# A hybrid conformer/attention trunk: layer norm statistics in two parts, a moved constant table, reordered silus and sums, and eight more taps on GpSimd

## The chip, the core and the metric

The kernel runs on one core of a Trainium2 chip. A core has five engines that each take their own instructions in order: TensorE (PE, matrix products), VectorE (DVE), ScalarE (ACT), GpSimd (POOL) and SyncE (SP, which here only issues transfers). They meet through semaphores, so an instruction that waits holds up everything behind it on its engine. The metric is the device time of one execution in microseconds, lower is better.

## What is computed

Two layers on a 512 x 1024 float32 activation. Layer 0 is a causal conformer convolution module and a SwiGLU feed-forward; layer 1 is sliding-window attention with shared keys and values and a second feed-forward; a final RMS norm follows. Only the convolution module and the start of the first feed-forward matter here:

```python
def conformer_conv(x, w_pw1, b_pw1, w_dw, b_dw, ln_g, ln_b, w_pw2, b_pw2):
    a = jax.nn.glu(x @ w_pw1 + b_pw1, axis=-1)
    y = lax.conv_general_dilated(
        a, w_dw[:, None, :].astype(a.dtype), window_strides=(1,),
        padding=((CONV_WIDTH - 1, 0),),
        dimension_numbers=('NWC', 'WIO', 'NWC'),
        feature_group_count=D_MODEL) + b_dw
    y = jax.nn.silu(layernorm(y, ln_g, ln_b))
    return y @ w_pw2 + b_pw2

h = h + conformer_conv(rmsnorm(h, norm_mix[l]), ...)
h = h + swiglu_ffn(rmsnorm(h, norm_ffn[l]), ffn_w_up[l], ffn_w_down[l])
```

The convolution is depthwise: each of the 1024 channels has 31 taps over the time axis. The layer norm goes over the 1024 channels. Layer 1's attention adds a relative-position bias, made from two small inputs (`sinks` and `rel_bias`).

## The kernel before

Channels lie on the 128 partitions in 8 channel tiles, tokens on the free axis. The convolution module is worked in two halves of 256 tokens (`hf` 0 and 1).

**The projection loop.** A `Pw1` (L546) is one channel tile of one half: 16 float32 matmuls of 256 columns (L555) into one PSUM bank, 8 for the linear part and 8 for the gate. After two tiles worked ahead, `projs` (L757) runs over the six remaining tiles of the first half (`at_` 0 to 5) and the eight of the second (`at_` 6 to 13). A tile's `gate` is a sigmoid on ACT (L564) and a product on DVE into the padded buffer `apad` (L569).

**The taps.** `Half.taps` (L579) convolves a tile. Of its 31 taps, `N_POOL` go the way ACT then POOL: ACT scales the shifted input into a buffer `pr` (first tap L594, others L596, eight buffers) and POOL adds it to the running sum (L597). The rest are multiply-adds on DVE (L602 for the first, L604). POOL adds the two sums into `y` (L608). Tiles are worked in four pairs (0 to 3); a step of `conv` is one DVE tap of both tiles of a pair with the ACT/POOL taps that fall to it.

**The statistics.** After pair 0, `shift_rows` (L621) forms a row of minus the mean of its channels with two matmuls (L624); it is the start of the DVE sum of later tiles, and is added to `y` of tiles 0 to 3 (L631). `squares` squares a pair's `y` on ACT (L633), `sums` adds `y` and its squares over partitions with four matmuls (L642). When all pairs are in, `scales` (L645) copies the sums on ACT (L647), turns them with four one-column matmuls (L650), forms mean and variance on DVE (L652 to L657), the power -0.5 on POOL (L659) and four diagonal blocks on ACT (L664); `spread` (L666) is one matmul that spreads them over the partitions (L668). `rows` (L670) then makes `z`: two DVE operations a tile (L680, L681) and a silu on ACT (L682).

**The order around it.** A list `follow` (L758) says after which projection what is issued. The first half's taps are spread over `at_` 0 to 10; from `at_` 10 on the second half's steps are taken early, `N_EARLY` (L527) of them a projection. The rest of the second half is a generator (`background`, L687), paid out as a `job` over the weight chunks of what follows: `pw2` (L707) of the first half, then its feed-forward `ffn_part`. `issue_after` fixes an earliest place in an issue order that a scheduler with its own timing then lays down; on the chip each engine follows that order.

**What follows on PE.** `pw2` is 64 float32 matmuls (L253), which take `z` tile by tile. Its evacuation gives `h` (L714) and the split input of the feed-forward, `x` as a high and a low part (L375 on ACT, L376 on DVE) with squares for the RMS norm (L329 on ACT, L333 on POOL). The feed-forward's products are three matmuls each (L255 to L257) with weights that are split as well: L203 on ACT (`whi`), L204 on DVE (`wlo`), from `raw` buffers that SP loads. Its RMS scale runs L343 on PE, L345 on DVE, L347 on POOL, L355 on ACT, L368 on PE.

**The bias constants.** `table` (L724) issues three small loads on SP's queue (`sk`, `lhs`, `oh`), a matmul (L730), two ACT operations (L731 on its result, L732 on `sk`) and a 3 MB store `fd`, which is read back much later for the attention bias.

Of the kernel before, what the change touches and what calls it, by code (L numbers as in the profile page):

```python
# [12 lines left out]
AF = mybir.ActivationFunctionType  # L13
ALU = mybir.AluOpType
# [21 lines left out]
LAST = (9, 11)  # L36
N_POOL = ((13, 13, 12, 12), (13, 17, 17, 17))

# [111 lines left out]
def hybrid_trunk(ctx: ExitStack, tc: tile.TileContext, xT, W, prm_in, wdw_in, sinks, relb, onehot, outT):  # L150
# [375 lines left out]
    N_RAW = 2  # L526
    N_EARLY = (5, 5, 8, 4)  # L527
    raw = [x[:, HALF[1]] for x in xg]
# [12 lines left out]
    with tc.tile_pool(name="conv", bufs=2) as cv:  # L541
# [29 lines left out]
        class Half:  # L571
            def __init__(self, hf, after=()):
                self.hf, self.after, self.last = hf, after, ()
                self.y = quads.tile([P, KT, W2], F32, tag="quad", name=uid("y"))
                self.shift = None
                self.st = None
                self.n_steps = sum(TAPS - n + 1 for n in N_POOL[hf]) + KT + 8

# [65 lines left out]

            def scales(self):  # L645
                row = temp()
                self.copied = nc.scalar.copy(row, self.st).ins  # L647
                pt = bank()
                for n in range(4):
                    nc.tensor.matmul(pt[:, n:n + 1], row[:, n * P:(n + 1) * P], ident[:, 0:1], start=n == 0, stop=n == 3)  # L650
                mv = small.tile([P, 2], F32, tag="mv", name=uid("mv"))
                nc.vector.tensor_scalar(mv, pt[:, 0:2], 1.0 / D, None, op0=ALU.mult)  # L652
                m2 = small.tile([P, 2], F32, tag="m2", name=uid("m2"))
                nc.vector.tensor_mul(m2, pt[:, 0:2], mv)
                nc.vector.tensor_sub(pt[:, 4:6], pt[:, 2:4], m2)
                var = small.tile([P, 2], F32, tag="var", name=uid("var"))
                nc.vector.tensor_scalar(var, pt[:, 4:6], 1.0 / D, EPS, op0=ALU.mult, op1=ALU.add)  # L657
                rr = small.tile([P, 2], F32, tag="rr", name=uid("rr"))
                nc.gpsimd.tensor_tensor(rr, var, mhalf[:, 0:2], op=ALU.pow)  # L659
                self.dg = temp()  # L660
                for n, c in enumerate((mv, rr)):
                    for e in range(2):
                        b = (2 * n + e) * P
                        self.spreads = nc.scalar.mul(self.dg[:, b:b + P], ident, c[:, e:e + 1]).ins  # L664
# [5 lines left out]
            def rows(self, split_z):  # L670
# [7 lines left out]
                for i in range(KT):  # L678
                    t = temp()[:, 0:W2] if split_z else self.z[i]
                    nc.vector.tensor_sub(t, self.y[:, i, :], pb[:, 0:W2])  # L680
                    nc.vector.tensor_mul(t, t, pb[:, W2:2 * W2])  # L681
                    nc.scalar.activation(t, t, AF.Silu, scale=col("lng", i), bias=col("lnb", i))  # L682
                    if split_z:
# [3 lines left out]
            def background(self):  # L687

                gen = self.conv()
                for p in range(KT // 2):  # L690
                    for _ in range(TAPS - N_POOL[self.hf][p] + 1):
                        next(gen)
                        yield
                    if p == 0:
                        self.shift_rows()
                        yield
                    self.squares(p)
                    yield
                    self.sums(p)
                yield  # L700
                self.scales()
                yield
# [20 lines left out]

        def table():  # L724
            nc.sync.dma_start(sk, sinks.to_broadcast([P, NH]))
            nc.sync.dma_start(lhs[0:NBUCKET, :], relb)
            nc.sync.dma_start(oh, onehot)
            nc.gpsimd.memset(lhs[NBUCKET:NBUCKET + 1, :], NEG)
            pf = bank()
            nc.tensor.matmul(pf[0:NH, 0:3 * P], lhs, oh, start=True, stop=True)  # L730
# [26 lines left out]
        projs = [(0, ct) for ct in range(N_RAW, KT)] + [(1, ct) for ct in range(KT)]  # L757
        follow = {2: [rms1.step1, table], 4: [lambda: norm_x(rms1, HALF[1]), h0.shift_rows]}  # L758
        for p, at_ in enumerate((5, 7, 9, 10)):
            follow.setdefault(at_, []).append(lambda p=p: h0.squares(p))  # L760
            follow.setdefault(at_ + 1, []).append(lambda p=p: h0.sums(p))
        follow[11].append(h0.scales)
        done, early, late = 0, 0, None
        for at_, (hf, ct) in enumerate(projs):
            proj = Pw1(hf, ct, mid=h0.spread if at_ == 13 else None)
            if late is not None:
# [4 lines left out]
            if hf == 0:  # L771
                proj.gate()
            while done < n_taps * min(1, (at_ + 1) / 11):
                next(taps, None)
                done += 1
            for f in follow.get(at_, ()):
                with tc.issue_after(proj.last[1 if f is h0.scales or at_ < 11 else 0]):
                    f()
# [3 lines left out]
            if at_ >= 10:  # L782

                with ExitStack() as st:
                    for ins in (gated, h0.copied if at_ == 12 else None, h0.spreads if at_ == 13 else None):
                        if ins is None:
                            continue
                        st.enter_context(tc.issue_after(ins))
                    for _ in range(N_EARLY[at_ - 10]):
                        next(second)  # L790
                        early += 1
        late.gate()
        for _ in h0.rows(False):
            pass
        base = seen[0]
        job(second, h1.n_steps - early, base, base + 44)
        x0 = {"ffn0": Act(KT)}
# [331 lines left out]
```

## Time and profile before

| | us |
|---|---|
| median of 3 runs | 1135.4 (1133.58 to 1135.97) |
| profiled execution | 1135.46 |
| its span, first to last instruction | 1133.7 |
| PE busy in the span | 1108.3 (98%) |
| DVE, ACT, POOL busy | 668.6, 512.2, 325.3 |
| PE idle in the span | 25.4 |
| mean granted PE clock | 0.993 |

1.8 us of the profiled execution lie outside its span. Times in the trace count from the span's start. In a timeline, rows of an engine give start, length, engine, line, operation, output and input, the count, and in brackets the idle time before with what ended it. In the view by windows, the count in brackets is of instructions that touch the window, and PEclk is the granted clock of TensorE as a share of full speed.

### The profile page before, as it was taken

What the parts mean: (1) busy time and instruction counts of PE and PEld (TensorE: products, weight loads), DVE (VectorE), ACT (ScalarE), POOL (GpSimd) and SP (SyncE); (2) the same over time, 40 slices, a digit from 0 to 9 for tenths busy, and PEclk for the clock granted to TensorE, in tenths of its full rate; (3) what the DMA queues carried; (4) which work ended last, traced back from release to release, by engine and by line L of the source; (5) the groups of instructions that cost most, each with busy time, mean ns of one, the idle gap of its engine ahead of it and who ended that gap; (6) DMA issues with size and microseconds to landing.
All of it is one profiled execution on the core that took longest, in us unless ns stands there. A gap on an engine that the chain in (4) does not pass through costs nothing.

```text
span 1133.7 us, 16111 instructions
## 1 busy us (share of the span) xinstructions
PE 1108.3 (98%) x6140; PEld 963.3 (85%) x6140; DVE 668.6 (59%) x1068; ACT 512.2 (45%) x902; POOL 325.3 (29%) x429
## 2 busy tenths in 40 slices
PE   9999898999999999999999999999999999999997
PEld 7888787899999998888878777888888888888887
DVE  4799788896865553454464675765444333444355
ACT  3787677845554433232352574643332212222234
POOL 3899689910010001121220232332111100111014
PEclk9999998999999999999999999999999999999998
DMA  9380034467555653333323211113323333233322
GB/s 362 105 97 4 9 106 165 133 203 242 171 184 185 186 175 105 93 93 101 103 75 99 85 41 38 38 56 98 107 93 93 97 106 95 93 93 97 108 91 97
DMA packets 41722, 128.16 MB, mean 113 GB/s; under 512 B 4491, under 2 KB 12844, under 8 KB 41644
## 3 DMA queue, kind: packets, MB, share of 16 engines
q1 hardware_dynamic: 40924, 126.56, 36.4%
q8 instruction: 48, 0.79, 0.3%
q10 hardware_dynamic: 720, 0.57, 0.2%
q14 instruction: 30, 0.25, 0.1%
HBM read 121.87 MB, written 5.24 MB: 112 GB/s over the span
## 4 chain that ended last, share of the span: by engine, by line
PE 77%; DVE 8%; issue 4%; ACT 4%; POOL 4%; DMA 3%; SPq 0%; POOLq 0%; DVEq 0%; ACTq 0%
PE bank L255 25%; PE bank L256 25%; PE bank L257 24%; DVE bank L604 4%; POOL pr L597 3%; PE bank L900 1%; ACT pr L596 1%; DMA w<-in_W_dram 1%; DVE quad L376 1%; DMA sk<-in_sinks_dram 1%; PE bank L921 1%; ACT whi L203 1%; DMA h<-in_xT_dram 1%; DVE wlo L204 1%; ACT z L682 0%
## 5 line engine op out<-in xcount | busy, mean ns | idle before, releaser
L256 PE MATMUL bank<-quad,whi 128*128 128x512 f32 (+1 forms) x1584 | 543.5, 343 | 2.4 <-DVE quad L376 2.4
L257 PE MATMUL bank<-quad,wlo 128*128 128x512 f32 (+1 forms) x1584 | 543.1, 343 | 1.8 <-DVE wlo L204 1.8
L255 PE MATMUL bank<-quad,whi 128*128 128x512 f32 (+1 forms) x1584 | 544.0, 345 | 0.3
L204 DVE TENSOR_TENSOR wlo<-raw,whi 128x1024 fp32r<-128x1024 f32 x200 | 269.8, 1349 | 318.5 <-ACT whi L203 309.7
L203 ACT CAST whi<-raw 128x1024 fp32r<-128x1024 f32 x200 | 209.6, 1048 | 361.8 <-PE bank L256 315.2
L256 PEld LDWEIGHTS bank<-quad,whi 128*128 128x128 f32 x1584 | 301.0, 190 | 38.6 <-DVE quad L376 3.7
L257 PEld LDWEIGHTS bank<-quad,wlo 128*128 128x128 f32 x1584 | 300.9, 190 | 36.8 <-DVE wlo L204 2.4
L255 PEld LDWEIGHTS bank<-quad,whi 128*128 128x128 f32 x1584 | 300.9, 190 | 36.5 <-ACT quad L939 0.6
L465 POOL TENSOR_TENSOR tmp<-tmp,tmp 128x512 f32<-128x512 f32 x32 | 45.6, 1427 | 485.1 <-DVE tmp L464 471.5
L597 POOL TENSOR_TENSOR pr<-pr,pr 128x256 f32<-128x256 f32 x212 | 161.0, 798 | 10.1 <-ACT pr L596 9.9
L604 DVE SCALAR_TENSOR_TENSOR bank<-apad,wdw,bank 128x256 f32<-128x256 f32 x244 | 113.6, 486 | 4.5
L555 PE MATMUL bank<-quad,w 128*128 128x256 f32 x512 | 113.7, 381 | 1.0 <-DMA w<-in_W_dram 0.7
L596 ACT ACTIVATE pr<-apad,wdw 128x256 f32<-128x256 f32 x212 | 102.3, 503 | 26.0 <-POOL pr L597 22.3
L555 PEld LDWEIGHTS bank<-quad,w 128*128 128x128 f32 x512 | 96.5, 190 | 17.0 <-DVE quad L530 3.2
L333 POOL TENSOR_TENSOR tmp<-tmp,tmp 128x256 f32<-128x256 f32 (+1 forms) x42 | 44.9, 1068 | 129.7 <-ACT tmp L329 103.6
L463 ACT ACTIVATE tmp<-tmp 128x512 f32<-128x512 f32 x32 | 20.1, 632 | 86.4 <-DVE tmp L462 86.4
L914 POOL TENSOR_SCALAR sc<-sc,sm 128x256 f32<-128x256 f32 (+1 forms) x64 | 30.6, 499 | 86.2 <-DVE sm L912 86.1
L376 DVE SCALAR_TENSOR_TENSOR quad<-h,prm,quad 128x512 fp32r<-128x512 f32 (+1 forms) x40 | 42.6, 1096 | 1.9 <-ACT quad L375 1.8
L379 ACT CAST quad<-tmp 128x512 fp32r<-128x512 f32 (+1 forms) x48 | 27.8, 585 | 29.5 <-POOL tmp L465 25.6
L464 DVE TENSOR_TENSOR tmp<-bank,rsbc 128x512 f32<-128x512 f32 x32 | 22.1, 691 | 30.4 <-PE bank L257 30.4
L910 ACT ACTIVATE sc<-sc,m 128x257 f32<-128x257 f32 (+1 forms) x64 | 30.2, 475 | 15.2 <-DVE m L903 14.5
L380 DVE TENSOR_TENSOR quad<-tmp,quad 128x512 fp32r<-128x512 f32 (+1 forms) x48 | 30.9, 651 | 2.3 <-ACT quad L379 2.3
(136 smaller groups left out, 754.3 us busy)
## 6 DMA issues: line engine op xcount, KB each, us to landing
raw<-in_W_dram SPq DMA_DIRECT2D x208, 512.0 KB, 3.5
w<-in_W_dram SPq DMA_DIRECT2D x15, 512.0 KB, 9.7
fd<-fs SPq DMA_DIRECT2D x1, 3072.0 KB, 33.8
h<-in_xT_dram SPq DMA_DIRECT2D x8, 256.0 KB, 5.6
bias<-fd SPq DMA_DIRECT2D x8, 256.0 KB, 5.7
out_dram<-res SPq DMA_DIRECT2D x13, 128.0 KB, 1.8
w<-in_W_dram SPq DMA_DIRECT2D x2, 256.0 KB, 4.0
out_dram<-res ACTq DMA_DIRECT2D x3, 128.0 KB, 2.4
```

Of the source, the lines that this page charges most:

```text
L203: nc.scalar.copy(hi, r)
L204: lo_engine[0].tensor_sub(lo, r, f32(hi))
L255: nc.tensor.matmul(out, w[0], x[0], start=start, stop=False)
L256: nc.tensor.matmul(out, w[0], x[1], start=False, stop=False)
L257: nc.tensor.matmul(out, w[1], x[0], start=False, stop=stop)
L333: self.eng.tensor_add(sq, self.acc, sq)
L376: nc.vector.scalar_tensor_tensor(dst[1], src, g, f32(dst[0]), op0=ALU.mult, op1=ALU.subtract)
L465: nc.gpsimd.tensor_mul(t2, t1, t2)
L555: mm = nc.tensor.matmul(self.pb[:, w * W2:(w + 1) * W2], w1[ct][:, w, k, :], x[k] if x else xg[k][:, tok], start=k == 0, stop=k == KT - 1)
L596: on_act = nc.scalar.mul(pr, a[:, j:j + W2], tap(j))
L597: on_pool = nc.gpsimd.tensor_add(pr, acc, pr)
L604: on_dve = nc.vector.scalar_tensor_tensor(yt if i == nd - 1 else c, src, tap(i), c if i else self.shift, op0=ALU.mult, op1=ALU.add)
```

## The change

It has five parts.

1. `table` is cut in two. `table_in` (the three loads and a memset) stays where `table` was, at `at_` 2; the matmul, the two ACT operations and the store move to `at_` 6, behind the sigmoid of the first half's last gate.
2. `scales` is cut into `scales_a` (copy, one-column matmuls, mean and variance) and `scales_b` (power and diagonal blocks), with second-half steps between; the `spread` comes ahead of all 16 matmuls of projection 13 and no longer between its halves.
3. The last gate of the second half moves behind the eight silus of the first half's `rows`, and the second half's further taps come behind them too.
4. In the second half, `shift_rows`, `squares` and `sums` of a pair are issued 3, 4 and 8 steps into the next pair, no longer at once; `N_EARLY` goes from (5, 5, 8, 4) to (7, 3, 4, 2), and the job's span from 44 to 42 weight chunks.
5. Pair 0 of the second half gives 17 taps a tile to ACT and POOL, before 13.

```diff
-N_POOL = ((13, 13, 12, 12), (13, 17, 17, 17))
+N_POOL = ((13, 13, 12, 12), (17, 17, 17, 17))
-    N_EARLY = (5, 5, 8, 4)
+    N_EARLY = (7, 3, 4, 2)
-            def scales(self):
+            def scales_a(self):
                 row = temp()
                 self.copied = nc.scalar.copy(row, self.st).ins
...
-                nc.vector.tensor_scalar(var, pt[:, 4:6], 1.0 / D, EPS, op0=ALU.mult, op1=ALU.add)
+                self.varied = nc.vector.tensor_scalar(var, pt[:, 4:6], 1.0 / D, EPS, op0=ALU.mult, op1=ALU.add).ins
+                self.mv, self.var = mv, var
+
+            def scales_b(self):
+                mv, var = self.mv, self.var
                 rr = small.tile([P, 2], F32, tag="rr", name=uid("rr"))
...
             def background(self):
                 gen = self.conv()
+                due = []
                 for p in range(KT // 2):
-                    for _ in range(TAPS - N_POOL[self.hf][p] + 1):
+                    for s in range(TAPS - N_POOL[self.hf][p] + 1):
                         next(gen)
+                        while due and due[0][0] <= s:
+                            due.pop(0)[1]()
                         yield
-                    if p == 0:
-                        self.shift_rows()
-                        yield
-                    self.squares(p)
+                    due = [(3, self.shift_rows)] if p == 0 else []
+                    due += [(4, lambda p=p: self.squares(p)), (8, lambda p=p: self.sums(p))]
+                for _, f in due:
+                    f()
                     yield
-                    self.sums(p)
+                self.scales_a()
                 yield
-                self.scales()
+                self.scales_b()
+                yield
                 yield
                 yield
                 self.spread()
                 yield from self.rows(True)
...
-        def table():
+        def table_in():
             nc.sync.dma_start(sk, sinks.to_broadcast([P, NH]))
             nc.sync.dma_start(lhs[0:NBUCKET, :], relb)
             nc.sync.dma_start(oh, onehot)
             nc.gpsimd.memset(lhs[NBUCKET:NBUCKET + 1, :], NEG)
+
+        def table():
             pf = bank()
...
-        follow = {2: [rms1.step1, table], 4: [lambda: norm_x(rms1, HALF[1]), h0.shift_rows]}
+        follow = {2: [rms1.step1, table_in], 4: [lambda: norm_x(rms1, HALF[1]), h0.shift_rows], 6: [table]}
...
-        follow[11].append(h0.scales)
+        follow[11].append(h0.scales_a)
         for at_, (hf, ct) in enumerate(projs):
-            proj = Pw1(hf, ct, mid=h0.spread if at_ == 13 else None)
+            if at_ == 13:
+                with tc.issue_after(proj.last[1]):
+                    spread = h0.spread()
+            with tc.issue_after(spread) if at_ == 13 else nullcontext():
+                proj = Pw1(hf, ct)
...
-                    for ins in (gated, h0.copied if at_ == 12 else None, h0.spreads if at_ == 13 else None):
+                    for ins in (gated, h0.copied if at_ == 11 else None, h0.varied if at_ == 11 else None, h0.spreads if at_ >= 12 else None):
...
+            if at_ == 11:
+                h0.scales_b()
-        late.gate()
         for _ in h0.rows(False):
             pass
+        with tc.issue_after(h0.silu):
+            late.gate()
+        h1.after = [h0.silu]
         base = seen[0]
-        job(second, h1.n_steps - early, base, base + 44)
+        job(second, h1.n_steps - early, base, base + 42)
```

More of the change, by code (lines that the diff above doesn't have):

```diff
@@ L576, in __init__ @@
                 self.st = None
-                self.n_steps = sum(TAPS - n + 1 for n in N_POOL[hf]) + KT + 8
+                self.n_steps = sum(TAPS - n + 1 for n in N_POOL[hf]) + KT + 7
             def taps(self, ct, c):
@@ L681, in rows @@
                     nc.vector.tensor_mul(t, t, pb[:, W2:2 * W2])
-                    nc.scalar.activation(t, t, AF.Silu, scale=col("lng", i), bias=col("lnb", i))
+                    self.silu = nc.scalar.activation(t, t, AF.Silu, scale=col("lng", i), bias=col("lnb", i)).ins
                     if split_z:
@@ L776, in hybrid_trunk @@
             for f in follow.get(at_, ()):
-                with tc.issue_after(proj.last[1 if f is h0.scales or at_ < 11 else 0]):
+                with tc.issue_after(last_sig) if f is table else nullcontext(), tc.issue_after(proj.last[1 if f == h0.scales_a or at_ < 11 else 0]):
                     f()
```

1 line of the change is left out of this document (added).

## The prediction

> **What bounds the kernel now.** I read the page, then the busy time by windows, then the timelines of each engine around the windows where PE is not full.
>
> ```profile
> span 1133.7 us, 16111 instructions
> PE 1108.3 (98%) x6140; PEld 963.3 (85%) x6140; DVE 668.6 (59%) x1068; ACT 512.2 (45%) x902; POOL 325.3 (29%) x429
> ...
> 260.00:600.00 340.00, 339.14 (x2132) 308.07 (x2132) 191.70 (x222) 138.56 (x183) 38.64 (x31) 1.00 0.45 142
> ...
> 770.00:1100.00 330.00, 330.00 (x1464) 273.19 (x1463) 135.84 (x143) 91.80 (x106) 31.73 (x23) 1.00 0.31 98
> ```
>
> The columns are PE, PEld, DVE, ACT, POOL, PEclk, DMA. PE is the bound; what the change touches ends near 275, and no matmul is added or removed. So only PE's idle time and lowered clock before that can be won, or grow:
>
> ```profile
> 50.00:60.00 10.00, 8.83 (x41) 7.12 (x40) 9.46 (x25) 8.52 (x19) 10.00 (x15) 1.00 0.58 67
> ...
> 130.00:140.00 10.00, 8.27 (x35) 6.12 (x34) 4.34 (x13) 9.04 (x16) 9.50 (x14) 1.00 0.01 2
> 140.00:150.00 10.00, 8.27 (x29) 6.34 (x29) 9.51 (x23) 9.99 (x23) 7.35 (x11) 0.83 0.23 73
> ...
> 170.00:180.00 10.00, 7.63 (x50) 6.38 (x48) 8.63 (x14) 9.17 (x21) 10.00 (x12) 0.92 0.68 256
> 180.00:190.00 10.00, 10.00 (x58) 9.51 (x58) 7.99 (x11) 6.25 (x11) 10.00 (x11) 0.74 0.36 107
> 190.00:200.00 10.00, 8.06 (x66) 7.80 (x65) 7.69 (x14) 7.21 (x14) 10.00 (x13) 1.00 0.33 106
> ...
> 230.00:240.00 10.00, 10.00 (x85) 10.00 (x85) 9.93 (x17) 4.30 (x6) 0.00 (x0) 1.00 0.68 200
> ```
>
> Idle is 1.2 (50 to 60), 3.5 (130 to 150), 2.4 (170 to 180) and 1.9 us (190 to 200); the lowered clock costs 10 x (1 - 0.83) = 1.7 us, and 0.8 + 2.6 = 3.4 us in 170 to 190. POOL is full from 170 on. The split matmuls go by at 10 / 85 = 0.118 us each.
>
> **Part 1, the constants.** The cause of the first gap is on ACT:
>
> ```profile
> 31.90 0.22 ACT L732 ACTIVATE sk<-sk 128x16 f32<-128x16 f32 x1 [7.01 <-DMA sk<-in_sinks_dram]
> ```
> ```profile
> 58.27 0.70 PE L624 MATMUL bank<-y,inv_s 128*128 128x256 f32 x2 [0.50 <-POOL y L608]
> 59.65 0.70 PE L624 MATMUL bank<-y,inv_s 128*128 128x256 f32 x2 [0.67 <-POOL y L608]
> ```
>
> The small L732 stands in ACT's queue ahead of the first taps and waits 7.01 us for a load that lies behind the weights in SP's queue. Behind it wait the taps, POOL's adds, the next sigmoid and so DVE. In the changed program's instruction order L732 and L731 stand behind the last first-half sigmoid, when the load has long landed. The taps then start 7 us earlier, `y` of pair 0 is there 7 us before PE asks, and 0.50 + 0.67 = **1.2 us** go. The moved matmul costs PE the same elsewhere. The store `fd` leaves some 25 us later, on a queue whose next weight load waits for a buffer until `pw2` runs: nothing. If the sigmoids, which wait for PE's projections, eat some of the 7 us, 1.2 us still fit. Bounds: 0 to 1.2; I take 1.2.
>
> **Parts 2 to 4 up to `pw2`.**
>
> ```profile
> 116.27 1.05 PE L650 MATMUL bank<-ident,tmp 128*128 128x1 f32 x8 [0.68 <-ACT tmp L647]
> ...
> 133.37 0.70 PE L624 MATMUL bank<-y,inv_s 128*128 128x256 f32 x2 [0.67 <-POOL y L608]
> 134.59 0.70 PE L642 MATMUL bank<-y,ones_m 128*128 128x256 f32 x2 [0.52 <-DVE y L631]
> 135.83 5.45 PE L253 MATMUL bank<-z,raw 128*128 128x256 f32 x24 [0.54 <-ACT z L682]
> 141.71 0.70 PE L253 MATMUL bank<-z,raw 128*128 128x256 f32 x2 [0.43 <-ACT z L682]
> 143.70 0.80 PE L642 MATMUL bank<-sq,ones_m 128*128 128x256 f32 x2 [1.30 <-ACT sq L633]
> ```
> ```profile
> 121.40 0.69 ACT L664 ACTIVATE tmp<-ident,mv 128x128 f32<-128x128 f32 x2 [5.18 <-DVE mv L652]
> ...
> 137.97 1.28 ACT L564 ACT_TABLE_LOAD   x1
> ...
> 139.76 1.28 ACT L682 ACT_TABLE_LOAD   x1
> ```
> ```profile
> 139.77 0.48 DVE L569 SCALAR_TENSOR_TENSOR apad<-bank,prm,tmp 128x256 f32<-128x256 f32 x1 [4.91 <-ACT tmp L564]
> ```
>
> All five gaps of 130 to 150 (3.46 us) come from `y` of the second half's pair 0 and from `z`. ACT stood 5.18 us at L664; later the last sigmoid cut into the silus, with two table loads, and DVE stood 4.91 us behind it with half of `z` unmade. Now in the new order:
>
> ```profile
> 19.64 22.61 PE L555 MATMUL bank<-quad,w 128*128 128x256 f32 x104
> ...
> 45.24 5.97 DVE L604 SCALAR_TENSOR_TENSOR bank<-apad,wdw,bank 128x256 f32<-128x256 f32 x15
> ```
> ```profile
> 145.39 13.20 POOL L597 TENSOR_TENSOR pr<-pr,pr 128x256 f32<-128x256 f32 x19 [0.16 <-ACT pr L596]
> ```
>
> A matmul of 256 columns is two records, 0.435 us; a DVE tap 0.40; a POOL add 0.695. PE ends L650 at about 116, does one projection (7.0), the spread (0.9) and another (7.0) and wants `z` at 130.9. The four small DVE operations now stand where DVE can only wait for L650, so the diagonals are there near 120, ahead of the spread at 123. DVE finishes pair 0's taps (eight fewer, 3.2 us) near 126, then makes a `z` every 1.1 us with a tap in between; ACT loads the silu table once and has the first `z` near 130. That leaves 1 us of slack at the start, and afterwards PE takes 1.74 us a tile against 1.1. The two L624 stand four and eight `pw2` matmuls in, L642 another 24: `y` (near 128) and its squares (near 140.5, behind silus and sigmoid) are in time for 132.6 and 145.7. So 3.5 us of waits and the clock loss behind them, 1.7, go: **5.2 us**. L650's 0.68 stays. Bounds: 2 us, if the first `z` is late by its slack and 1.7 stays, to 5.2.
>
> **The start of the feed-forward.**
>
> ```profile
> 156.23 4.70 DVE L376 SCALAR_TENSOR_TENSOR quad<-h,prm,quad 128x256 fp32r<-128x256 f32 x1 [1.49 <-ACT quad L375]
> ```
> ```profile
> 162.69 0.79 POOL L333 TENSOR_TENSOR tmp<-tmp,tmp 128x256 f32<-128x256 f32 x1 [2.05 <-issue]
> ...
> 168.83 9.31 POOL L597 TENSOR_TENSOR pr<-pr,pr 128x256 f32<-128x256 f32 x10
> ...
> 196.25 17.20 POOL L597 TENSOR_TENSOR pr<-pr,pr 128x256 f32<-128x256 f32 x19
> ```
> ```profile
> 172.79 0.39 PE L257 MATMUL bank<-quad,wlo 128*128 128x256 f32 x1 [0.72 <-DVE wlo L204]
> ...
> 176.73 0.39 PE L256 MATMUL bank<-quad,whi 128*128 128x256 f32 x1 [0.93 <-DVE quad L376]
> ...
> 197.05 0.70 PE L368 MATMUL bank<-tmp,ones_m 128*128 128x256 f32 x2 [1.94 <-ACT tmp L355]
> ...
> 215.17 0.70 PE L642 MATMUL bank<-y,ones_m 128*128 128x256 f32 x2 [1.23 <-POOL y L608]
> ```
>
> The first L376 took 4.70 us, about ten times a tap, and ended when POOL fell idle (the 2.05 before L333). DVE was late by 4 us from there, and PE paid 2.4 us in 170 to 180 and then 3.4 of clock. In the changed order DVE has pair 1's taps behind it before the first L376 (near 146), and POOL, empty after the silus, meets its first wait for a square near 147: the same pause, ten microseconds ahead of need. I count those 5.8 us as won.
>
> The Trainium skill ("SBUF — State Buffer", "Who interferes with whom") says that a DVE instruction with two SBUF inputs and a GpSimd instruction that reads SBUF exclude each other for one whole instruction. By that, L376 could be held for one add, 0.7 us, and this gain would shrink to what the late L204 cost, 0.72: a sum of 1132. The row shows 4.70, six adds long, so the measurement decides.
>
> Against it stands **part 5** and the silu block. ACT gives POOL no taps from its table load near 128 until the last sigmoid near 137.5; then POOL has, by the instruction order, 72 instructions to the first `y` of pair 2. PE starts the feed-forward at 130.9 + 64 x 0.435 + 2.6 (L624, L642) = 161.3 and asks for that `y` after 242 split matmuls (28.6 us) and 2.5 us of small ones: 192.4. POOL does 34 by 161.3 at 0.695; the other 38, beside L204, go at 0.92 (0.93 and 0.905 in its two rows): 196.3. PE waits 3.9 us, shared between L368 and L642, for 3.17 before: +0.7. At 0.695 throughout there is no wait (-3.2); at 0.93 throughout it is 12.1 (+8.9); 0.92 beside the weight splits is the nearest row. Of the rest: the square of pair 1 stands ahead of weight splits on ACT, and the last `x` tiles are made as PE asks, 0.6; the second half's L650 now stands directly behind the last L642, where 26 matmuls stood between, so PE waits for ACT's copy as at 116.27, 0.8 (0 to 2.5); and 1.5 for a clock that reacts to the new waits (0 to 3.4). DVE's eight taps are worth 3.2 us only where DVE is late, and the silu table load at the first feed-forward evacuation costs ACT 1.28 us where its casts run two chunks ahead: nothing, or 1.28 if that lead is gone.
>
> **Sum**, against the profiled execution's 1135.46 (span 1133.7; the runs' median is 1135.4): -1.2 - 5.2 - 5.8 + 0.7 + 0.6 + 0.8 + 1.5 = -8.6, so **1127 us**.
>
> **The rivals.**
> *POOL keeps up.* With adds nearer to 0.695, the 3.2 us of POOL's waits go and none follow: 1135.46 - 1.2 - 5.2 - 5.8 - 3.2 + 0.8 = 1120.9. For it: fewer splits fall into POOL's stretch. Against: every row after 168 is at 0.9.
> *The clock does not follow the waits.* If its two dips come at their own time, 1.7 + 3.4 stay and the 1.5 falls away: 1130.6. Against: both dips begin within 2 us of a cluster of gaps; for it: 1.94 us before L368 brought none. The Trainium skill ("TensorE: Matmul & The Clock Gate", "HAM oscillation") ties the lowered clock to idle gaps over about 3.4 us; no gap here is over 1.94, so by that rule the dips are not these waits' doing, though the trace has them behind smaller ones.
> *POOL becomes the bound.* Adds at 0.93 from 137.5 on give +8.9 for +0.7: 1135.2, no change. The silu block and eight more adds (5.6 us) speak for it; the 0.695 while DVE has one SBUF input speaks against.
> *DVE is held by POOL, again and again: slower.* The changed POOL order has unbroken runs of 12, 17 and 31 adds. Where L204 meets such a run as L376 did, each hold costs 4.2 us (4.70 less a usual 0.5). With three that PE sees, 1127 + 12.6 = 1139.6; from the second on the 8.6 are used up. Against: in 170 to 230 many L204 ran among runs of 10 and 19 adds, and POOL's 0.92 shows that they took turns.
>
> **How the numbers follow.** Forecast 0.60 (own range 1124 to 1130), POOL keeps up 0.15, clock stays 0.10, POOL bound 0.07, DVE held 0.08. About 0.2%, 2.3 us, is what a measurement can tell from no change. Faster: 0.60 + 0.15 + 0.10 = 0.85; same 0.07; slower 0.08. The range leaves out those last two, and the far end of the first rival: 1121 to 1133.
>
> **What would show it.** ACT without a 7 us wait near 25 to 32, and no gap before L624 near 57; one silu table load with eight silus behind it, and `pw2` from about 131 without a gap over 0.5; PEclk 1.00 in 140 to 150; the feed-forward's first split matmul near 161; no L376 of 4 us that PE waits for; waits at L368 and pair 2's L642 of about 4 us together, and a new one at the second L650. I am wrong if the first split matmul comes after 165, or if waits between 165 and 275 come to over 15 us with the clock loss.

## The result and the profile after

| | before | after |
|---|---|---|
| median of the runs, us | 1133.58 (1133.29 to 1135.97, 5 runs) | 1130.33 (1129.07 to 1130.66, 5 runs) |
| profiled execution, us | 1135.46 | 1130.66 |
| its span, us | 1133.7 | 1128.9 |
| ratio after to before | | 0.9963, 95% interval 0.9951 to 0.9974 |

The changed kernel is 3 us faster, 4.8 us between the two profiled executions; forecast were 8.6 us and 1127. The runs of the kernel before fall into two groups: of the 52 taken beside the experiments below, 25 lie between 1132.95 and 1134.43 us and 27 between 1135.08 and 1137.23, at the same mean granted clock of 0.993, and its profiled execution, 1135.46, belongs to the upper one. The page of the changed kernel, its first lines:

```profile
span 1128.9 us, 16125 instructions
...
PE 1103.1 (98%) x6140; PEld 960.1 (85%) x6140; DVE 660.7 (59%) x1060; ACT 515.0 (46%) x910; POOL 334.6 (30%) x437
```

PE does the same 6140 matmuls in 5.2 us less. That is the clock, as the windows of the changed kernel show (PE, PEld, DVE, ACT, POOL, then PEclk):

```profile
0.00:20.00 20.00, 16.70 (x74) 13.68 (x75) 5.16 (x13) 5.06 (x12) 7.58 (x28) 1.00 0.92 336
50.00:60.00 10.00, 10.00 (x48) 8.81 (x47) 9.26 (x22) 8.01 (x17) 10.00 (x15) 1.00 0.00 0
...
130.00:150.00 20.00, 20.00 (x94) 17.60 (x94) 16.35 (x40) 16.71 (x38) 12.01 (x17) 1.00 0.34 106
160.00:180.00 20.00, 17.32 (x127) 16.12 (x127) 17.32 (x27) 16.56 (x34) 20.00 (x23) 1.00 0.52 179
180.00:200.00 20.00, 17.09 (x137) 16.44 (x136) 16.39 (x26) 15.54 (x30) 20.00 (x23) 1.00 0.41 131
200.00:240.00 40.00, 35.91 (x279) 34.18 (x279) 36.33 (x49) 31.17 (x57) 34.85 (x36) 1.00 0.47 156
240.00:260.00 20.00, 19.32 (x155) 18.76 (x154) 10.88 (x15) 9.01 (x13) 1.29 (x3) 1.00 0.79 247
```

The idle time of 50 to 60 and of 130 to 150 is gone, and no window has a lowered clock. From 160 to 260 PE is idle for 2.7 + 2.9 + 4.1 + 0.7 = 10.4 us; in the kernel before it was 6.6 there. The timeline of PE names these waits (the first row is the feed-forward's first split matmul, without a wait):

```profile
161.35 0.47 PE L255 MATMUL bank<-quad,whi 128*128 128x256 f32 x1
...
168.16 0.39 PE L256 MATMUL bank<-quad,whi 128*128 128x256 f32 x1 [0.59 <-DVE quad L376]
...
170.59 0.39 PE L256 MATMUL bank<-quad,whi 128*128 128x256 f32 x1 [0.94 <-DVE quad L376]
...
178.18 0.61 PE L343 MATMUL bank<-ones_c,tmp 128*128 128x1 f32 x4 [1.15 <-POOL tmp L333]
...
186.42 0.70 PE L368 MATMUL bank<-tmp,ones_m 128*128 128x256 f32 x2 [1.77 <-ACT tmp L355]
...
197.13 0.38 PE L257 MATMUL bank<-quad,wlo 128*128 128x256 f32 x1 [1.14 <-DVE wlo L204]
...
200.61 0.39 PE L255 MATMUL bank<-quad,whi 128*128 128x256 f32 x1 [0.59 <-ACT whi L203]
...
216.31 0.39 PE L257 MATMUL bank<-quad,wlo 128*128 128x256 f32 x1 [0.99 <-DVE wlo L204]
...
220.76 0.39 PE L257 MATMUL bank<-quad,wlo 128*128 128x256 f32 x1 [1.32 <-DVE wlo L204]
...
227.73 0.39 PE L257 MATMUL bank<-quad,wlo 128*128 128x256 f32 x1 [0.65 <-DVE wlo L204]
...
250.50 1.05 PE L650 MATMUL bank<-ident,tmp 128*128 128x1 f32 x8 [0.68 <-ACT tmp L647]
```

New against before are above all the waits for split weights from 197 on: with a 0.38 at 202.28 they are 5.07 us, against 0.43 + 0.64 from 190 on before. L642 of pair 2 no longer waits. On ACT the wait for the constants is gone, and the taps start at 26.4 instead of 32.6:

```profile
25.77 0.71 ACT L329 ACTIVATE tmp<-h 128x256 f32<-128x256 f32 x2
26.39 0.59 ACT L594 ACTIVATE pr<-apad,prm,wdw 128x256 f32<-128x256 f32 x1
```

### The profile page after: what moved, and what is told of

Its sections match the earlier page's. It is cut to its first block, busy times and chain, and to the rows that moved or that the text cites. A ratio compares the mean times of both kernels' runs of the same rounds, so it can differ in the third digit from the quotient of the medians.

```text
span 1128.9 us, 16125 instructions
## 1 busy us (share of the span) xinstructions
PE 1103.1 (98%) x6140; PEld 960.1 (85%) x6140; DVE 660.7 (59%) x1060; ACT 515.0 (46%) x910; POOL 334.6 (30%) x437
## 4 chain that ended last, share of the span: by engine, by line
PE 85%; DVE 5%; issue 5%; POOL 2%; ACT 2%; DMA 1%; SPq 0%; POOLq 0%; ACTq 0%; DVEq 0%
PE bank L255 24%; PE bank L256 24%; PE bank L257 24%; PE bank L555 8%; POOL pr L597 2%; PE bank L919 1%; DVE bank L604 1%; PE bank L940 1%; DVE quad L376 1%; PE bank L642 1%; DVE wlo L204 1%; ACT whi L203 1%; DMA h<-in_xT_dram 1%; ACT pr L596 0%; DVE sc L922 0%
## 5 line engine op out<-in xcount | busy, mean ns | idle before, releaser
L256 PE MATMUL bank<-quad,whi 128*128 128x512 f32 (+1 forms) x1584 | 542.6, 343 | 2.4 <-DVE quad L376 2.4
L204 DVE TENSOR_TENSOR wlo<-raw,whi 128x1024 fp32r<-128x1024 f32 x200 | 271.4, 1357 | 326.0 <-ACT whi L203 317.6
L203 ACT CAST whi<-raw 128x1024 fp32r<-128x1024 f32 x200 | 209.6, 1048 | 357.8 <-PE bank L256 306.5
L256 PEld LDWEIGHTS bank<-quad,whi 128*128 128x128 f32 x1584 | 300.2, 189 | 38.2 <-DVE quad L376 3.4
L597 POOL TENSOR_TENSOR pr<-pr,pr 128x256 f32<-128x256 f32 x220 | 170.5, 812 | 14.0 <-ACT pr L596 13.7
L596 ACT ACTIVATE pr<-apad,wdw 128x256 f32<-128x256 f32 x220 | 105.3, 503 | 27.1 <-POOL pr L597 25.3
L604 DVE SCALAR_TENSOR_TENSOR bank<-apad,wdw,bank 128x256 f32<-128x256 f32 x236 | 108.5, 485 | 3.6
L376 DVE SCALAR_TENSOR_TENSOR quad<-h,prm,quad 128x512 fp32r<-128x512 f32 (+1 forms) x40 | 39.2, 1011 | 1.9 <-ACT quad L375 1.7
```

The source lines that it names most:

```text
L203: nc.scalar.copy(hi, r)
L204: lo_engine[0].tensor_sub(lo, r, f32(hi))
L256: nc.tensor.matmul(out, w[0], x[1], start=False, stop=False)
L376: nc.vector.scalar_tensor_tensor(dst[1], src, g, f32(dst[0]), op0=ALU.mult, op1=ALU.subtract)
L596: on_act = nc.scalar.mul(pr, a[:, j:j + W2], tap(j))
L597: on_pool = nc.gpsimd.tensor_add(pr, acc, pr)
```

## The experiments

The waits of PE between 155 and 240 and the loss to a lowered clock between 100 and 300 are read from each kernel's own profile; the medians are of runs beside runs of the kernel before on the same chip. The median of these lay between 1133.6 and 1135.4, so versions from different chips are better compared by the ratio.

| kernel | median, us | ratio to before, 95% interval | waits 155 to 240 | of these for weights | clock |
|---|---|---|---|---|---|
| before | 1133.58 | | 6.5 | 1.8 | 5.1 |
| changed | 1130.33 | 0.9963, 0.9951 to 0.9974 | 9.5 | 5.1 | 0 |
| e8: changed, again | 1130.62 | 0.9964, 0.9951 to 0.9976 | 9.4 | 5.0 | 0 |
| e1: constants alone | 1128.67 | 0.9953, 0.9936 to 0.9971 | 7.4 | 0 | 1.7 |
| e6: one multiplication moved | 1128.29 | 0.9945, 0.9932 to 0.9958 | 7.4 | 0 | 1.7 |
| e7: changed without the constants | 1131.19 | 0.9971, 0.9962 to 0.9981 | 8.2 | 3.8 | 1.7 |
| e4: gate between the silus | 1129.83 | 0.9960, 0.9946 to 0.9975 | 7.5 | 5.2 | 1.7 |
| e3: sums not delayed | 1131.19 | 0.9968, 0.9955 to 0.9980 | 10.7 | 5.0 | 0 |
| e2: pair 0 at 13 taps | 1129.15 | 0.9950, 0.9937 to 0.9963 | 8.5 | 3.3 | 1.7 |
| e5: pairs 2, 3 at 15 taps | 1129.58 | 0.9953, 0.9939 to 0.9967 | 8.2 | 2.3 | 3.4 |
| e9: steps over 46 chunks | 1129.79 | 0.9952, 0.9938 to 0.9965 | 9.4 | 5.6 | 1.7 |
| c1: e1, pairs 1 to 3 at 15 taps | 1130.44 | 0.9971, 0.9959 to 0.9983 | 8.1 | 3.9 | 1.7 |
| e10: e6, squares added on DVE | 1134.85 | 1.000, 0.999 to 1.001 | 10.8 | 4.1 | 5.1 |
| e11: e6, steps over 46 chunks | 1130.26 | 0.9959, 0.9946 to 0.9971 | 8.0 | 2.0 | 3.4 |

### The constants alone, down to one instruction

In the kernel before, `table` was cut as in the change and nothing else (e1):

```diff
-        follow = {2: [rms1.step1, table], 4: [...]}
+        follow = {2: [rms1.step1, table_in], 4: [...], 6: [table]}
```

> The kernel before with the constants alone moved (the three loads stay, the matmul and the two small ACT operations come behind the last first-half sigmoid). Theory (the 7.01 us wait on ACT was the cause of the two gaps before L624): ACT has no such wait, the 0.50 and 0.67 us gaps near 58 are gone, nothing else changes, 1.2 us less: 1133.58 - 1.2 = 1132.4. The run also answers for the clock: from 130 on its program is that of before. If the two clock dips (0.83 in 140 to 150, 0.92 and 0.74 in 170 to 190) hang on the gaps, they come again behind the same gaps; rival, if the clock has its own time: with the same gaps the dips are elsewhere or missing, and the time differs by up to 5.1 us from run to run.

Then only the multiplication of `sk`, 0.2 us on ACT, was moved; loads, matmul and store stayed (e6):

```diff
-            nc.scalar.mul(sk, sk, -1.0)
...
         late.gate()
+        with tc.issue_after(late.sig):
+            nc.scalar.mul(sk, sk, -1.0)
```

> The kernel before with one ACT instruction moved: the 0.22 us multiplication of sk, which waited 7.01 us for its load, stands behind the last sigmoid of the second half; loads, table matmul and store stay where they were. Theory (the wait itself, carried by ACT, POOL and DVE from 25 to past 155, is what the whole change won): the taps start 7 us earlier, the first silu table load near 128.5 where it was at 133.9, and the time is that of the constants moved whole, 1128.7 (five to six under before). Rival (the moved matmul, evacuation and store of the table have a share): 1130 to 1132.

And the other side, the changed kernel with `table` whole and at `at_` 2 again (e7), beside the changed kernel once more (e8):

```diff
-        follow = {2: [rms1.step1, table_in], 4: [...], 6: [table]}
+        follow = {2: [rms1.step1, table], 4: [...]}
```

> The changed kernel with the constants back where they were: statistics in two parts, silus ahead of the last gate, later sums and the eight taps more on POOL, and the 7 us wait on ACT as before. Theory (the constants carry the gain, the rest at most hides a part of the same lateness): the wait's 1.2 us at L624 near 58 and most of the lateness to 120 are back; the two-part statistics are worth something here only because they take the small DVE operations out of the tap queue: between 1131 and 1134, so at least 1 us over the changed kernel. Rival (the prediction as it stands: parts 2 to 4 and the feed-forward's start win 5.2 + 5.8 - 3.6 by themselves): 1130.3 + 1.2 = 1131.5 at most and 1130 at best, with no lowered clock in 140 to 150. They part at the wait before L624 and L253 in 130 to 150: over 2 us by the theory, none by the rival.

> The changed kernel once more, beside the others on the same chip. Theory: 1129 to 1131, 1 to 2 us over the constants alone, since the rest brings 3 us of waits more between 190 and 230 (weight splits) for 0.6 less in 130 to 140. The lowered clock is read here too: if it comes in pieces of 3.41 us at half speed (1.71 us each, as in all profiles so far) that start at a time of their own, this profile has none, one or two of them, behind a window of 3.41 us with at least 1.3 us idle.

My estimate for e1, 1132.4, was far off: 1128.67, and e6 with one instruction 1128.29. No run of e6 (1127.85 to 1129.15) is as slow as the fastest of e8 (1129.35) on the same chip. The timelines of ACT and PE and the windows of e6 show why:

```profile
25.82 0.70 ACT L329 ACTIVATE tmp<-h 128x256 f32<-128x256 f32 x2
...
129.35 1.28 ACT L682 ACT_TABLE_LOAD   x1
```
```profile
132.80 0.70 PE L642 MATMUL bank<-y,ones_m 128*128 128x256 f32 x2 [0.51 <-DVE y L631]
...
180.64 0.61 PE L343 MATMUL bank<-ones_c,tmp 128*128 128x1 f32 x4 [0.88 <-POOL tmp L333]
...
190.25 0.70 PE L368 MATMUL bank<-tmp,ones_m 128*128 128x256 f32 x2 [3.15 <-ACT tmp L355]
...
208.35 0.70 PE L642 MATMUL bank<-y,ones_m 128*128 128x256 f32 x2 [1.24 <-POOL y L608]
```
```profile
130.00:150.00 20.00, 19.33 (x89) 16.39 (x88) 16.77 (x40) 19.15 (x40) 16.76 (x26) 1.00 0.27 80
...
180.00:200.00 20.00, 16.21 (x119) 15.96 (x120) 15.45 (x22) 15.44 (x30) 20.00 (x23) 0.91 0.40 128
200.00:240.00 40.00, 38.76 (x316) 38.33 (x316) 35.99 (x52) 27.39 (x44) 22.77 (x24) 1.00 0.54 172
```

With the wait of ACT gone the first silu table load comes at 129.4, where it was at 133.9, with the sigmoid still cutting into the silus. PE is idle for 0.67 us in 130 to 150 instead of 3.46, at full clock. So what e6's profile lacks are the two waits at L624 near 58 (1.2 us), 2.8 us in 130 to 150, and two of the three windows of lowered clock (3.4 us); the waits from 155 to 240 are 7.4 us, no fewer than the 6.5 before. So the lateness that I read as the order's doing in 115 to 145 was the 7 us from ACT's wait at 25: POOL and DVE were nearly full behind it (10.00 and 9.46 of 10 us in the window 50 to 60) and could not make it up, and PE shows it only where it wants `y` and `z`.

e7 has that wait again (its rows on ACT and PE, and two windows):

```profile
32.22 0.22 ACT L740 ACTIVATE sk<-sk 128x16 f32<-128x16 f32 x1 [7.47 <-DMA sk<-in_sinks_dram]
```
```profile
58.60 0.70 PE L624 MATMUL bank<-y,inv_s 128*128 128x256 f32 x2 [0.95 <-POOL y L608]
59.97 0.70 PE L624 MATMUL bank<-y,inv_s 128*128 128x256 f32 x2 [0.67 <-POOL y L608]
```
```profile
130.00:140.00 10.00, 10.00 (x48) 8.82 (x47) 8.69 (x25) 6.88 (x12) 1.97 (x4) 1.00 0.18 54
140.00:150.00 10.00, 10.00 (x48) 8.80 (x48) 7.90 (x16) 9.47 (x25) 10.00 (x15) 1.00 0.47 156
```

Its waits at L624 are 1.6 us, and none follow to 150: for this run my theory (over 2 us in 130 to 150) fell and the rival held: no wait there, full clock, 1131.2. Both sets of numbers are true at once: the two parts of the change remove the same idle time. Each wins alone, the moved multiplication 5.4 us (1133.70 to 1128.29) and the rest 2.5 (1133.70 to 1131.19); together they win 3.1 (to 1130.62), so the rest costs 2.3 us by the medians once the multiplication is moved. The waits in the profile of the changed kernel, against e6: 0.7 less in 130 to 140, 2.9 less before L256, L343, L368 and L642 together (1.53 + 2.92 against 2.10 + 5.27), 5.1 more for split weights and 0.7 more at the second L650, in sum 2.2. But e6's profile has 1.7 us of lowered clock that this one lacks, and on the chip of e6 and e8 the two profiled executions are only 0.5 us apart (1129.15, the longest of e6's runs, and 1129.65). So the profiles show where the waits went, but not the whole 2.3 us.

### What makes the split weights late

Five edits of the changed kernel each take away one suspect. The last gate ahead of the silus in the program's order, which puts it behind three of the eight silus (e4):

```diff
+        late.gate()
         for _ in h0.rows(False):
             pass
-        with tc.issue_after(h0.silu):
-            late.gate()
```

> The changed kernel with the last gate ahead of the silus again: ACT does three silus, loads the sigmoid table, the gate, loads the silu table, and the other five silus, so no load is left for L456 in the feed-forward. Theory (the third load at 195.39 is one of the causes of the late weight casts there: 1.14 and 0.59 us before L257 and L255 at 197 and 200): those two shrink, but ACT's taps start 1.3 us later and the silus are made in 3 us more: PE has 4.4 us of slack at the fourth z, so no wait there; in all 1130.3 - 1.7 + 1 = 1129.6. Rival (the order of silus and gate is what won the 5.2 us): waits before L253 and a lower clock in 140 to 150 come back, 1133 or more.

Squares and sums without delay (e3):

```diff
-                    due += [(4, lambda p=p: self.squares(p)), (8, lambda p=p: self.sums(p))]
+                    due += [(0, lambda p=p: self.squares(p)), (0, lambda p=p: self.sums(p))]
```

> The changed kernel without the delay: squares and sums of a pair of the second half come directly behind its last step, not four and eight steps later; statistics, silus and taps as changed. Theory (with the constants moved y is early anyway in pw2, and only in the feed-forward does the delay hide POOL's last add): no wait in pw2 or one of at most 0.5, L642 of pairs 1 and 2 waits again, 1.2 us each as in the kernel with the constants alone: 1130.4 + 1.5 = 1132. Rival (the delay is worth the 1.30 us of the square before L642 at 143.70 as well): 1133 or more. If it changes nothing, PE's waits at L642 were only another place for the same lateness of POOL: 1130.4.

Fewer taps for POOL in pair 0 (e2) or in pairs 2 and 3 (e5), and a thinner stream of steps (e9):

```diff
-N_POOL = ((13, 13, 12, 12), (17, 17, 17, 17))
+N_POOL = ((13, 13, 12, 12), (13, 17, 17, 17))
```
```diff
+N_POOL = ((13, 13, 12, 12), (17, 17, 15, 15))
```
```diff
-        job(second, h1.n_steps - early, base, base + 42)
+        job(second, h1.n_steps - early, base, base + 46)
```

> The changed kernel with pair 0 of the second half back at 13 taps on POOL (eight adds fewer on POOL, eight taps more on DVE). Theory (POOL's backlog is what the feed-forward waits for; ACT's weight casts L203 stand behind taps that wait for a buffer from POOL): POOL is 8 x 0.92 = 7 us earlier, the 9.5 us of waits in 160 to 240 fall by 2 to 3, 1130.3 - 2.5 = 1127.8. Rival (DVE is what is late there, 89% busy in 200 to 240): eight DVE taps more are 3.2 us, y of pair 0 and the weight splits come later, up to 1133.

> The changed kernel with pairs 2 and 3 of the second half at 15 taps on POOL instead of 17 (eight adds fewer for POOL, eight taps more for DVE, both in 185 to 240). Theory (POOL's backlog): the waits from 197 to 228 (1.14, 0.59, 0.38, 0.99, 1.32, 0.65, together 5.1 us) halve, 1130.3 - 2.5 = 1127.8. Rival (DVE is late, its splits are slow beside POOL): 3.2 us more on DVE, waits before L257 grow by 1 to 3, 1132.

> The changed kernel with the second half's background steps paid out over 46 weight chunks instead of 42. In the changed kernel 44 of its 59 steps are taps, so they are through after 44/59 x 42 = 31.3 chunks; in the kernel before it was 49 of 58 steps in 44 chunks, 37.2; here it is 34.3. Theory (the taps come too densely after 160: ACT's weight casts and DVE's splits stand behind taps that wait for POOL): the waits for weights from 195 to 230, 5.05 us in the changed kernel, shrink by half, 1130.4 - 2.5 = 1128. Rival (the waits are the price of the 17 taps of pair 0 on POOL and of the third table load, not of the pace): unchanged within 0.6, 1130.

The rows behind the first of these waits (197.13 in the changed kernel) show who waits for whom: ACT's tap L596 for a buffer from POOL, behind it the cast L203, DVE's L204 for that cast, and PE for L204 (ACT, then DVE):

```profile
193.23 0.51 ACT L596 ACTIVATE pr<-apad,wdw 128x256 f32<-128x256 f32 x1 [0.86 <-POOL pr L597]
...
194.34 1.03 ACT L203 CAST whi<-raw 128x1024 fp32r<-128x1024 f32 x1
```
```profile
195.41 1.67 DVE L204 TENSOR_TENSOR wlo<-raw,whi 128x1024 fp32r<-128x1024 f32 x1 [0.44 <-ACT whi L203]
```

The kernel before has such a wait of ACT as well (0.84 us at 203.83) and pays less for it, so the chain alone does not say why there is more of it now. e4 has no load at L456, and its waits for weights are 5.2 us, where they were 5.1; the first of them:

```profile
196.22 0.39 PE L257 MATMUL bank<-quad,wlo 128*128 128x256 f32 x1 [1.16 <-DVE wlo L204]
```

So the third table load is not their cause, nor is it the order of gate and silus that won anything at PE: with it undone no wait came back in 130 to 150. The pace is not the cause either (5.6 us in e9, where I had expected half), nor the delay of the sums (5.0 in e3; what the delay hides is one wait of 1.87 us before L642 at 168). Only fewer taps on POOL bring them down, to 3.3 in e2 and 2.3 in e5, and then L343 (2.81) or L642 (1.21 and 1.81) wait for POOL instead. None of e2, e5 and e9 gained the 2.5 us that I expected (by the ratios 1.1 to 1.6 us, with intervals that overlap the changed kernel's), and the sum of the waits stays between 6.5 and 10.8 us in all fourteen profiles. What is left of the suspects is the silu block itself, in which POOL gets no taps (changed kernel, POOL):

```profile
138.61 10.73 POOL L597 TENSOR_TENSOR pr<-pr,pr 128x256 f32<-128x256 f32 x15 [7.99 <-ACT pr L596]
```

In e6 that pause is 2.80 us, and pair 1 is through on POOL at 159.7 against 167.8. That is argued from the rows; the block was not tried alone, and in e2 pair 1 comes later still with fewer waits. It stays open.

### Versions built on the constants alone

e1 with (13, 15, 15, 15) taps (c1), e6 with the seven additions of squares on DVE (e10), e6 with 46 chunks (e11):

```diff
+N_POOL = ((13, 13, 12, 12), (13, 15, 15, 15))
```
```diff
         n0 = Next(("ffn0",), x0, bc0, HALF[0])
+        n0.rms = Rms(bc0, HALF[0])
+        n0.rms.eng = nc.vector
```
```diff
-        job(second, h1.n_steps - early, base, base + 44)
+        job(second, h1.n_steps - early, base, base + 46)
```

> The kernel before with the constants moved, and pairs 1 to 3 of the second half at 15 taps on POOL instead of 17. What is left there are waits of POOL's making: 0.87 us before L343, 3.15 before L368, 1.22 before L642. Theory (POOL is the late engine from 150 to 210): 12 adds fewer are 11 us of POOL at 0.92, these 5.2 us go and nothing comes for them as DVE still waits for ACT there: 1128.7 - 4 = 1124.7. Rival (twelve DVE taps more, 5 us, make DVE late, as it was with 17 taps in pair 0): waits before L256 and L257 take their place, 1128 to 1130.

> The kernel before with the multiplication of sk moved, and the seven additions of squares for the first feed-forward's RMS norm (L333) on DVE instead of POOL. Theory (what is left in the feed-forward are POOL's chains: 0.88 us before L343, 3.15 before L368, 1.24 before L642, behind tap adds): DVE pays 7 x 0.42 = 3 us where it has idle time before L204, POOL is 5 to 6 us earlier: L343's and L642's waits go, L368's falls to 1 at most, and the lowered clock behind them may stay away: 1128.3 - 4 = 1124.3. Rival (L368 waits for the power L347, which still stands behind tap adds in POOL's queue, and DVE has no idle time to give): within 1 us of 1128.3.

> The kernel before with two edits: the multiplication of sk moved, and the second half's steps paid out over 46 weight chunks instead of 44 (taps through after 49/58 x 46 = 38.9 chunks instead of 37.2). Theory (POOL's chains set the waits left, 0.88 before L343, 3.15 before L368, 1.24 before L642, and a thinner stream of taps shortens them, as L368's wait fell from 1.77 to 0.22 us when the changed kernel went from 42 to 46): L368's wait falls by 1.5, 1128.3 - 1.5 = 1126.8. Rival (the sums of pairs come later with it and the last part of the work is moved into waits further on, as 46 chunks moved 2 us of the changed kernel's waits to 225 to 232): 1128.3 within 0.7.

None is faster than what it was built on; the medians are 1.8, 6.6 and 2.0 us higher, though on other chips, and for c1 and e11 the intervals overlap with those of e1 and e6. In c1 the wait at L368 falls from 3.15 to 0.23 us (L343's grows from 0.87 to 2.08), and waits for weights of 1.48 and 0.63 at 163 and 167 take its place, as the rival said. Whether for its reason is open: in c1 the first L376 is also held by POOL for 4.79 us (see the last section), which it is not in e1, and e11, which has the taps of e6 and a hold of 4.69 us, has waits at the same two places. e10 shows the price of handing POOL's work to DVE (groups of instructions by line in 140 to 200, e10 first, then e6; the last numbers are busy us and mean ns):

```profile
L333 DVE TENSOR_TENSOR tmp<-tmp,tmp 128x256 f32<-128x256 f32 x7 | 5.6, 795 | 0.0
```
```profile
L333 POOL TENSOR_TENSOR tmp<-tmp,tmp 128x256 f32<-128x256 f32 x7 | 6.5, 922 | 0.0
```

I had reckoned with 0.42 us each; beside POOL most took 0.95. L642 of pair 2 waited 3.2 us instead of 1.2, and the clock was lowered three times (here, too, the first L376 was held, for 4.01 us). e11's L368 wait fell by 0.4, not 1.5, and waits of 0.77 and 1.18 for weights at 163 and 167 are new. e6, the kernel before with one instruction moved, has the lowest median of all. Its interval overlaps with those of all versions but e7, e10 and c1, so that it is the best is shown only beside the changed kernel, by the runs on one chip (e8).

## Why the prediction was right in sum, and where its steps were not

The time, 1130.33, lies in the whole range of 1121 to 1133, 3.3 us over the 1127 and just outside the 1124 to 1130 that the forecast itself was given. The gain was 4.8 us between the profiles and 3.2 between the medians, where 8.6 was forecast. That it is no further off is in part luck: between the profiles, three parts cost 6.3 us more than forecast (the weights, the start of the feed-forward, the first 20 us), and others 2.5 us less (the clock, POOL). The number is also that of the rival in which the clock's dips stay and no new one comes (1130.6), but in this profile none stayed.

- **The constants, 1.2 us.** Their two gaps went as said, but this is the step that failed. "If the sigmoids ... eat some of the 7 us, 1.2 us still fit. Bounds: 0 to 1.2" takes the 7 us as paid off within the first half. They are not: one instruction of them alone is worth 5.4 us (e6). The upper bound had to be what the lateness costs wherever it next meets PE.
- **Up to `pw2`, 5.2 us.** Right in place and size: 3.46 us of gaps and 1.7 of clock are gone, `pw2` starts at 131.3 (forecast 130.9). The reason was half right. The order of silus, gate and statistics does remove these gaps (e7), but so does the moved multiplication alone (e6, all but 0.67), and ACT's 5.18 us before L664 and DVE's 4.91 were mostly that wait, 100 us downstream: in e6 they are 1.34 and 2.17 us. I credited one cause with a gain for which two stood.
- **The feed-forward's start, 5.8 us.** 161.35 was forecast to 0.1 us, and the 3.4 us of clock came. Of the 2.4 us of idle time only 0.8 went: waits for L376 between 166 and 180 (0.95 to 2.56 us) are there in every kernel, with a held first L376 or without. So the hold of 4.70 us that I gave them to is not their cause; these tiles are made while PE asks.
- **POOL late, +0.7.** L343, L368 and pair 2's L642 wait 2.92 us against 3.17 before, so -0.2 (L368 alone 1.77 and L642 nothing, where about 4 were forecast, but L343 1.15 where there was no wait): it is not POOL's own results that come late.
- **What was missing** is the split weights. I allowed 0.6 us for the last `x` tiles and a square ahead of the casts, and 5.07 us of waits for L203 and L204 came in place of 1.07. That is 3.4 us of the error. That it is POOL's backlog seen through taps ahead of these casts is argued from the rows at 193 to 197 and from e2 and e5, not shown.
- **The second L650, +0.8**: measured 0.68. **The clock's reaction, +1.5**: none in this profile; for what is known of it see below. **Table load at L456, 0**: right (e4).

Measured against the forecast's terms: -1.2 - 5.2 - 4.2 - 0.2 + 4.0 + 0.7 = -6.1, and +1.3 for the first 20 us, where PE waits for its first loads and nothing was changed: -4.8, the difference of the profiles. The 1.3 is chance: e8, the same program, is idle for 2.23 us there and not for 3.30, and the fourteen profiles for 1.6 to 3.3. The window of the kernel before, with 17.98 us busy against 16.70:

```profile
0.00:20.00 20.00, 17.98 (x78) 14.56 (x79) 6.46 (x15) 5.06 (x12) 7.56 (x28) 1.00 0.94 342
```

**The rivals.** POOL did not keep up, nor did it become the bound by its own results. DVE was not held again and again: the longest L204 is 1.82 us, and the first L376 took 0.68. That the clock has its own time was half true.

## What to carry to other kernels

A short instruction that waits at the head of a full queue costs what its lateness costs where it next meets the bound, not what the next gap shows (here 5.4 us for an instruction of 0.22 us, where the next gaps showed 1.2); follow it until an engine has had idle time to catch up. When two parts of a change could each remove the same gap, their gains do not add, and only a run of each alone tells which one pays. Where three engines beside PE are near full, shifting work between them moved the waits from one line to another here: their sum stayed between 6.5 and 10.8 us in every version, and no shift brought it below that of the kernel before.

## What the runs showed of the hardware

**The lowered clock comes on a grid of 3.41 us.** In one-microsecond windows of the kernel before (last columns PEclk, DMA share, GB/s):

```profile
144.00:145.00 1.00, 1.00 (x4) 0.80 (x3) 0.93 (x3) 1.00 (x3) 0.80 (x2) 0.58 0.00 0
145.00:146.00 1.00, 1.00 (x3) 0.74 (x3) 0.93 (x3) 1.00 (x3) 0.84 (x2) 0.50 0.00 0
146.00:147.00 1.00, 1.00 (x4) 0.82 (x3) 0.93 (x3) 1.00 (x4) 1.00 (x3) 0.50 0.00 0
147.00:148.00 1.00, 1.00 (x5) 0.86 (x4) 0.93 (x3) 1.00 (x4) 0.92 (x2) 0.71 0.00 0
```

The clock is halved for 0.84 + 2 + 0.58 = 3.42 us, which costs 1.71. All sixteen dips between 100 and 300 in the fourteen profiles last 3.41 us, but for one of twice that. Two dips of one profile lie whole numbers of 3.413 us apart: 34.13 us (10) in the kernel before, 17.07 and 17.06 (5) in e5 and e11, 10.24 and 37.55 (3 and 11) in e10. In the 3.41 us ahead of each dip PE was idle for 1.27 to 3.20 us, so all stand behind a cluster of waits. But idle time in a window of the grid does not decide it alone. These two windows, of the kernel before and of e3, were followed by full clock:

```profile
195.37:198.78 3.41, 1.73 (x13) 1.68 (x14) 2.35 (x5) 2.98 (x7) 3.41 (x6) 1.00 0.47 154
```
```profile
184.05:187.47 3.41, 1.65 (x15) 1.44 (x13) 2.97 (x4) 2.33 (x7) 3.41 (x5) 1.00 0.18 73
```

PE was idle for 1.68 and 1.77 us in them. In e5 (183.79 to 187.21) and e7 (185.18 to 188.59) the same 1.77 us before L368 were followed by a dip. (e3 has no dip in this stretch; its grid is laid from the lowering at its end, 1122.72, 275 windows behind the start of this one. In the kernel before, the lowering at the end lies on the grid of its dips too, 276 windows behind the second.) In the changed kernel a border of the grid, at 185.22, cuts the wait before L368 into 0.56 and 1.21 us, which may be why it has no dip, but e3's wait lies whole in one window and has none either. What else decides is open. The count of dips differs between profiles, and 1.7 us each is as large as most differences sought here. The Trainium skill ("TensorE: Matmul & The Clock Gate", "What's actually happening") says that the clock is halved after an idle window of 3413 ns, and that these windows run free of the kernel. Length, half and free run agree with these traces; but here windows that were idle for 1.27 us, little over a third, were enough at times, and one with 1.77 us was not.

**DVE can lose to POOL for a whole run of adds.** The first L376 of the feed-forward, in e11 (DVE, then POOL) and in e6, whose code differs there in nothing but the pace of the steps:

```profile
150.79 4.69 DVE L376 SCALAR_TENSOR_TENSOR quad<-h,prm,quad 128x256 fp32r<-128x256 f32 x1 [2.10 <-ACT quad L375]
```
```profile
139.95 13.20 POOL L597 TENSOR_TENSOR pr<-pr,pr 128x256 f32<-128x256 f32 x19 [0.16 <-ACT pr L596]
153.10 0.74 POOL L333 TENSOR_TENSOR tmp<-tmp,tmp 128x256 f32<-128x256 f32 x1
153.78 1.42 POOL L597 TENSOR_TENSOR pr<-pr,pr 128x256 f32<-128x256 f32 x2
157.25 0.78 POOL L333 TENSOR_TENSOR tmp<-tmp,tmp 128x256 f32<-128x256 f32 x1 [2.05 <-issue]
```
```profile
151.80 0.58 DVE L376 SCALAR_TENSOR_TENSOR quad<-h,prm,quad 128x256 fp32r<-128x256 f32 x1 [2.09 <-ACT quad L375]
```
```profile
140.96 13.39 POOL L597 TENSOR_TENSOR pr<-pr,pr 128x256 f32<-128x256 f32 x19 [0.16 <-ACT pr L596]
154.30 0.91 POOL L333 TENSOR_TENSOR tmp<-tmp,tmp 128x256 f32<-128x256 f32 x1
155.18 1.59 POOL L597 TENSOR_TENSOR pr<-pr,pr 128x256 f32<-128x256 f32 x2
```

In e11 POOL goes on at its undisturbed 0.7 us an add, and L376 ends when POOL has run dry; in e6 both pass, and the POOL instructions beside this L376 and the next two take 0.91 or 0.92 us each, 0.2 more than usual. Seven of the fourteen profiles have such a hold of 4.0 to 4.8 us (before, c1, e3, e5, e9, e10, e11), always at the first L376, and seven have 0.58 to 0.68. With the splits L204 POOL does take turns: in e6 the L204 at 160.25 takes 1.23 us, and the POOL addition begun at 160.34 takes 1.72 us and not 0.73. The Trainium skill ("SBUF — State Buffer", "Who interferes with whom") has the two engines exclude each other for one instruction; here it was six adds or one. A hold costs DVE some 4 us, and what decides it is open: it is not where in a POOL add L376 begins, as in e11 and in e6 alike that was 0.43 us behind the add's start, and no program here has one profile with the hold and one without (the changed kernel's two have none). That the hold is what sets the runs of one program apart was not shown either.
